# An opening gather of 128 slots instead of 256 in each expert layer, with the expert sort dealt out between its blocks

## The chip, the core and the metric

The program runs on one NeuronCore of a Trainium2 chip. The metric is the device time of one execution in microseconds (us), the median of several runs. Five engines work side by side: TensorE (PE, with its weight loads PEld), VectorE (DVE), ScalarE (ACT), GpSimd (POOL) and SyncE (SP), which issues nearly all DMA transfers.

## The reference, cut to what matters

The model has two transformer layers with attention and a mixture of experts, and then a third block of another kind. The change touches the two expert layers only. Layer 0 has 512 tokens, layer 1 has 256. Each token goes to 2 of 32 experts.

```python
grp   = argmax(g_logits)                         # one of 4 groups
top_p, top_i = top_k(softmax(e_logits[grp]), 2)  # two experts of that group
gate  = p_grp * top_p / sum(top_p)
...
xb = h_pad[slot_tok]                             # rows of tokens, expert by expert
yb = (silu(xb @ w1[e]) * (xb @ w3[e])) @ w2[e]   # D=1024, FF=512, float32
out[stok] += yb[dest] * sgate
```

The weights of an expert are 6 MB (w1, w3 and w2 of 2 MB each), and every expert is read once per layer: 192 MB a layer.

## The kernel before, in words

**Units.** `moe(l, Tn, ob)` handles one expert layer, with Tn = 4 or 2 tiles of 128 tokens. The 32 experts are packed into 14 units of 128 token slots: a unit of two experts has 64 slots for each, a unit of four has 32 for each. Units 0 and 1 hold the experts 0 to 3, which are fixed (`FIX = 4`). The experts of units 2 to 13 are placed by load: `sort_experts` ranks them by the number of their tokens, and the resulting ids (`eid`) are read by SP (`eid_at`, L862) to form the addresses of their weights. Unit 2 has four experts.

**Weights.** `Stream` lists 1 MB tiles in the order of use: w1 and w3 of unit 0 (8 tiles), w1 and w3 of unit 1 (8), w2 of unit 0 (4), w1 and w3 of unit 2 (16), w2 of unit 1 (4), and so on. They go through a ring of 12 tiles in layer 0 and 17 in layer 1. SP issues them in this order from L302; a tile can be issued when the tile that held its place has been multiplied. So the first tile whose address needs the sort is the 21st.

**Gather.** The rows of tokens are fetched by a product with a one-hot matrix: `onehot_tok(base)` writes `gr` (token x 256 slots, type fp32r), and `gather` multiplies it with the tokens `hs`, split into two fp32r parts `hi` and `lo`. The result is `xt`, 8 slices k of 128 features x 256 slots. For each k there are Tn x 2 matmuls with 128x128 weights (from `hs`) and 256 moving columns (from `gr`), accumulated in one PSUM bank for two slices, and ScalarE copies each bank to `xt` (L1100). One gather serves two units.

**The opening.** Before the first unit, `gather(gr0, blocks=(0, 1))` fills k = 0 to 3 for both units 0 and 1. `up` (L1216) multiplies `xt` with w1 of unit 0, slice by slice; in its middle, at k = 4, it calls the gather of k = 4 to 7 (pinned there by `late`). Then comes `overflow_slots`, a generator: its first part counts the tokens of each expert (L1157), runs `sort_experts` (L1136 to L1152) and stops at its `yield`; then `up` with w3 of unit 0; then its second part computes the final slots (L1165 to L1181). Units 1 to 13 follow, each with `up` for w1 and w3, and `down` (w2) and `combine` of the unit before it. Units 2, 4, 6, ... begin with a gather of 256 slots.

**Order.** The instructions of an engine run in program order. A planner makes that order from the order in which they are written and from its own estimate of when each is ready; `pin` fixes places by hand.

Of the kernel before, what the change touches and what calls it, by code (L numbers as in the profile page):

```python
# [163 lines left out]
def build(tc, A, out, stages=("A0", "M0", "A1", "M1", "F", "B"), dbg=None, inject=None):  # L164
# [22 lines left out]
    with es:  # L187
# [24 lines left out]
        def pin(i, on=True):  # L212
            return tc.keep_in_program_order(i) if on and i is not None else i
# [216 lines left out]
        def fill(n=1):  # L430
            for _ in range(n):
                if fills:
                    fills.pop(0)()
# [377 lines left out]
        def moe(l, Tn, ob):  # L811
# [78 lines left out]
            with sbuf(f"ringx{l}", nX, "right") as ringX, ExitStack() as mid, ExitStack() as early, ExitStack() as main:  # L890
# [13 lines left out]
                def sm(*shape, dt=F32, pool=M_):  # L904
                    cnt[0] += 1
                    return pool.tile([128] + list(shape), dt, name=f"s{cnt[0]}")
# [180 lines left out]
                        V.scalar_tensor_tensor(gr[:, t], C("iota"), sh[:, 1, t:t + 1], gr[:, t].bitcast(F32), op0=OP.is_equal, op1=OP.add)  # L1087
                    return gr

                def gather(gr, n=256, blocks=range(4), late=False):  # L1090
                    for b in blocks:
                        ps = PS()
                        for kk in range(2):
                            k = 2 * b + kk
                            o = ps[:, n * kk:n * kk + n]
                            for t in range(Tn):
                                h = hs[t // 2][:, t % 2, k]
                                pin(T.matmul(o, h.hi, gr[:, t, :n], start=(t == 0), stop=False), late and kk == t == 0)
                                T.matmul(o, h.lo, gr[:, t, :n], start=False, stop=(t == Tn - 1))
                        S.copy(xt[:, 2 * b:2 * b + 2, :n], ps[:, :2 * n].rearrange("p (k s) -> p k s", k=2))  # L1100

                gr0 = onehot_tok(0)
                gather(gr0, blocks=(0, 1))
                fill(100)
                W.pools, W.n = ringM, stream.done
                stream.upto(n2 + RN)

                gate, ex, den, ge, pg = sm(2, Tn), sm(Tn), sm(Tn), sm(Tn, 4), sm(Tn)
                pin(V.tensor_tensor(ge, g, gm[:, :, None].to_broadcast([128, Tn, 4]), op=OP.subtract))
                S.activation(ge, ge, AF.Exp)  # L1110
                V.tensor_reduce(pg, ge, axis=AX.X, op=OP.add)
                V.reciprocal(pg, pg)
                V.tensor_sub(m2, m2, m1)
                V.tensor_mul(m2, m2, gf)
                V.tensor_reduce(ex, m2, axis=AX.X, op=OP.add)
                S.activation(ex, ex, AF.Exp)
                V.tensor_scalar(den, ex, 1.0, None, op0=OP.add)
                V.reciprocal(den, den)
                V.tensor_mul(gate[:, 0], pg, den)
                V.tensor_mul(gate[:, 1], gate[:, 0], ex)  # L1120

                rowt = ob.tile([128, 2, 2, N], F32, name="rowt", tag="o")
                grow = sm(nC, D, pool=Z_)
                for c in range(nC):
                    modrow(grow[:, c], l, 5, c)

                cntc, ovc, cmp_, ovb = sm(1), sm(1), sm(nj), sm(3, 32)
                eid = lbx[:, 0:32].bitcast(I32)
# [4 lines left out]
                def sort_experts():  # L1133
                    T_ = C("tab")
                    ones, idn = C("ones"), ident[0:32, 0:32]
                    V.tensor_scalar(key[0:32], cntc[0:32], T_[0:32, 2:3], T_[0:32, 3:4], op0=OP.mult, op1=OP.add)  # L1136
                    pr = PS()
                    T.matmul(pr[0:32, 0:32], key[0:32].to_broadcast([32, 32]), idn, start=True, stop=True)
                    V.tensor_scalar(gt_[0:32], pr[0:32, 0:32], key[0:32], None, op0=OP.is_lt)
                    pr = PS()  # L1140
                    T.matmul(pr[0:32, 0:32], ones[0:32, 0:32], gt_[0:32], start=True, stop=True)
                    T.matmul(pr[0:32, 32:34], gt_[0:32], ones[0:32, 0:2], start=True, stop=True)
                    V.tensor_scalar(oh[0:32, 0], pr[0:32, 0:32], C("pcol")[0:32], None, op0=OP.is_equal)
                    V.tensor_scalar(oh[0:32, 1], C("iota32")[0:32], pr[0:32, 32:33], None, op0=OP.is_equal)
                    pr = PS()
                    T.matmul(pr[:, 0:32], C("pcol")[0:32].to_broadcast([32, 128]), oh[0:32, 1], start=True, stop=True)
                    for i in range(2):
                        T.matmul(pr[:, 32 + 32 * i:64 + 32 * i], T_[0:32, i:i + 1].to_broadcast([32, 128]), oh[0:32, 0], start=True, stop=True)
                    T.matmul(pr[0:32, 96:98], oh[0:32, 0], T_[0:32, 1:2].to_broadcast([32, 2]), start=True, stop=True)
                    V.tensor_copy(eid[0:1], pr[0:1, 0:32])  # L1150
                    V.tensor_copy(tabs, pr[:, 32:96].rearrange("p (a b) -> p a b", a=2))
                    V.tensor_copy(capc[0:32], pr[0:32, 96:97])  # L1152

                def overflow_slots():
                    pc = PS()
                    for t in range(Tn):
                        T.matmul(pc[0:32, 0:2], at_[:, t], C("ones")[:, 0:2], start=(t == 0), stop=(t == Tn - 1))  # L1157
                    V.tensor_copy(cntc[0:32], pc[0:32, 0:1])
                    sort_experts()
                    V.tensor_sub(cntc[0:32], cntc[0:32], capc[0:32])  # L1160
                    for j in range(nj):
                        V.tensor_scalar(cmp_[0:32, j:j + 1], cntc[0:32], float(128 * j), None, op0=OP.is_gt)
                    V.tensor_reduce(ovc[0:32], cmp_[0:32], axis=AX.X, op=OP.add)
                    yield
                    po = PS()  # L1165
                    for i, m in enumerate(("tri", "ident", "ones")):
                        T.matmul(po[:, 32 * i:32 * i + 32], ovc[0:32].to_broadcast([32, 128]), C(m)[0:32, 0:32], start=True, stop=True)
                    V.tensor_copy(ovb, po[:, 0:96].rearrange("p (a b) -> p a b", a=3))
                    V.tensor_sub(ovb[:, 0], ovb[:, 2], ovb[:, 0])
                    V.tensor_sub(ovb[:, 0], ovb[:, 0], ovb[:, 1])  # L1170
                    bx = gt_
                    V.tensor_scalar(bx, ovb[:, 0], 128.0, float(OVF), op0=OP.mult, op1=OP.add)
                    V.tensor_sub(bx, bx, tabs[:, 1])
                    pick(ek, tabs[:, 0, None, None, :].to_broadcast(wide))
                    pick(ovr, tabs[:, 1, None, None, :].to_broadcast(wide))
                    V.tensor_tensor(ovr, pk, ovr, op=OP.is_ge)
                    V.tensor_add(slot, ek, pk)
                    pick(bk, bx[:, None, None, :].to_broadcast(wide))
                    V.tensor_sub(bk, bk, ek)
                    V.tensor_mul(bk, bk, ovr)  # L1180
                    V.tensor_add(slot, slot, bk)  # L1181
                    debug(f"slot{l}", slot)

                def gate_rows():
                    for a, src in enumerate((slot, gate)):
# [20 lines left out]
                    V.scalar_tensor_tensor(sr, rowt[:, 0, 1], sid, s0, op0=OP.is_equal, op1=OP.add)  # L1206
                    return sr, gt[:, 2]

                def up(off, ws, mid=lambda: None):
                    ps = PS()  # L1210
                    m = 128 // len(ws)
                    for k in range(8):
                        if k == 4:
                            mid()
                        for q, w in enumerate(ws):
                            T.matmul(ps[m * q:m * q + m, :], xt[:, k, off + m * q:off + m * q + m], at(w, k)[k],  # L1216
                                     start=(k == 0), stop=(k == 7))
                    return ps
# [120 lines left out]
                for i in order + [None]:  # L1339
                    if i is not None:  # L1340
                        off = 128 * (i % 2)
                        if off == 0 and i != 0:
                            gather(onehot_tok(128 * i))
                        if i == 0:
                            p1 = up(off, ws[i][0], lambda: gather(gr0, blocks=(2, 3), late=True))
                            ov = overflow_slots()
                            next(ov)
                            p3 = up(off, ws[i][1])
                            next(ov, None)
                        if i > 1:  # L1350
                            sr, gt = scatter_mats(128 * i, i == last)
                        if i != 0:
                            p1 = up(off, ws[i][0])
                        if i == 1:
                            gate_rows()
                            pend[2:4] = scatter_mats(0)[::-1]
                            sr, gt = scatter_mats(128)
# [776 lines left out]
```

## Time and profile before

| | |
|---|---|
| median of 3 runs | 2079.9 us (2075.26 to 2083.57) |
| the profiled execution, its own time | 2082.3 us |
| its span, first to last instruction | 2080.6 us |
| mean granted TensorE clock | 0.975 |
| PE busy | 1944.3 us (93%) |
| DVE busy | 1076.9 us (52%) |
| ACT busy | 658.5 us (32%) |
| POOL busy | 475.8 us (23%) |
| moved by DMA | 585.44 MB |

The expert stage of layer 0 lies at about 318 to 780 us of the span, that of layer 1 at about 1051 to 1500. In a row of instructions the first number is the start in us, the second the duration, followed by engine, line, operation, result <- operands, shape and count; in brackets stands the idle time before it and what ended it. A float32 matmul appears as two records, an fp32r matmul as one. In a row of windows, each engine has its busy time and, in brackets, its instructions; then follow the granted clock (1.00 is 2.4 GHz, 0.50 is 1.2 GHz), the busy share of the 16 DMA engines, and GB/s.

### The profile page before, as it was taken

To read this page: it belongs to the slowest core of one execution; us is meant where nothing else is said; L and a number is where in the kernel's file an instruction comes from. 1 tells how busy PE (TensorE), PEld (TensorE's weight loads), DVE (VectorE), ACT (ScalarE), POOL (GpSimd) and SP (SyncE) were. 2 spreads that over 40 slices of the span, in tenths; PEclk is the share of its full clock that TensorE was granted. 3 is DMA by queue.
4 is the path that set the end of the run, shared out by engine and by line. 5 is a ranking of instruction groups with operands and counts; after the bars stand their busy time and mean duration, and the time that the engine had idled before them with its cause. 6 is when DMAs were issued, how large, how long until landed. Compare 5 with 4: busy or idle time off the path is not lost. (4 is left out here: it accounts for less than half of the span.)

```text
span 2080.6 us, 29614 instructions
## 1 busy us (share of the span) xinstructions
PE 1944.3 (93%) x11353; PEld 1229.8 (59%) x11353; DVE 1076.9 (52%) x1919; ACT 658.5 (32%) x1188; POOL 475.8 (23%) x365
## 2 busy tenths in 40 slices
PE   6999999999899998999899997999989999998997
PEld 3755574444344444677743332333379998988996
DVE  3476674454426566746643231233366775446553
ACT  3355531101001114446511010111164444455553
POOL 1234321121213123210111010011131440332331
PEclk7999999999999999999899999999999999999999
DMA  8573338999999996642389999999864453554552
GB/s 316 209 258 128 102 134 339 398 427 426 427 426 425 427 423 251 246 142 102 132 364 427 426 427 427 426 426 427 370 223 135 146 182 129 183 192 142 183 189 95
DMA packets 137794, 585.44 MB, mean 281 GB/s; under 512 B 17257, under 2 KB 21863, under 8 KB 88367
## 3 DMA queue, kind: packets, MB, share of 16 engines
q1 hardware_dynamic: 136798, 583.47, 71.8%
q8 instruction: 92, 1.51, 0.3%
q14 instruction: 56, 0.45, 0.1%
q10 hardware_dynamic: 848, 0.01, 0.0%
HBM read 582.33 MB, written 1.11 MB: 280 GB/s over the span
## 5 line engine op out<-in xcount | busy, mean ns | idle before, releaser
L1216 PE MATMUL ps<-w,xt 128*64 128x512 f32 (+1 forms) x2232 | 430.1, 612 | 23.7 <-DMA w<-expert_w 23.4
L269 DVE TENSOR_TENSOR spl<-w,sph 128x1024 fp32r<-128x1024 f32 (+1 forms) x153 | 203.8, 1335 | 193.8 <-ACT sph L266 192.7
L266 ACT CAST sph<-w 128x1024 fp32r<-128x1024 f32 (+1 forms) x204 | 213.0, 1045 | 282.0 <-PE pj L260 258.2
L1216 PEld LDWEIGHTS ps<-w,xt 128*64 128x64 f32 (+1 forms) x2232 | 125.6, 127 | 276.0 <-issue 225.1
L1271 DVE SCALAR_TENSOR_TENSOR t<-ps,gt,t 128x512 fp32r<-128x512 f32 x52 | 39.1, 751 | 474.7 <-ACT t L1270 473.0
L1255 PE MATMUL ps<-w,t 128*64 128x512 f32 (+1 forms) x1128 | 257.1, 604 | 16.3 <-DMA w<-expert_w 13.5
L1287 POOL TENSOR_TENSOR X<-X,tm 128x512 f32<-128x512 f32 x78 | 106.1, 1360 | 687.8 <-DVE tm L1286 686.5
L259 PE MATMUL pj<-hT2h,sph 128*128 128x256 f32 x864 | 241.0, 283 | 0.0
L260 PE MATMUL pj<-hT2l,sph 128*128 128x256 f32 x864 | 240.4, 280 | 0.0
L261 PE MATMUL pj<-hT2h,spl 128*128 128x256 f32 x864 | 239.2, 281 | 0.3 <-DVE spl L269 0.3
L269 POOL TENSOR_TENSOR spl<-w,sph 128x1024 fp32r<-128x1024 f32 (+1 forms) x51 | 126.5, 2481 | 340.1 <-ACT sph L266 339.7
L1270 ACT ACTIVATE t<-ps,gt 128x512 fp32r<-128x512 f32 x52 | 35.7, 687 | 515.6 <-PE ps L1255 513.0
L1255 PEld LDWEIGHTS ps<-w,t 128*64 128x64 f32 (+1 forms) x1128 | 82.2, 125 | 183.1 <-issue 131.9
L260 PEld LDWEIGHTS pj<-hT2l,sph 128*128 128x128 f32 x864 | 163.0, 189 | 0.8 <-issue 0.7
L259 PEld LDWEIGHTS pj<-hT2h,sph 128*128 128x128 f32 x864 | 162.3, 189 | 1.2 <-issue 0.7
L261 PEld LDWEIGHTS pj<-hT2h,spl 128*128 128x128 f32 x864 | 161.7, 188 | 0.6 <-DVE spl L269 0.5
L1280 PE MATMUL ps<-t,sr 128*128 128x512 f32 x336 | 96.0, 415 | 9.2 <-DVE t L1271 7.5
L1286 DVE TENSOR_TENSOR tm<-ps,s 128x512 f32<-128x512 f32 x156 | 101.9, 680 | 1.4 <-PE ps L1280 1.3
L1280 PEld LDWEIGHTS ps<-t,sr 128*128 128x128 f32 x336 | 60.1, 188 | 57.4 <-ACT t L1270 22.3
L445 PEld LDWEIGHTS ps<-c,t 128*128 128x128 f32 x496 | 56.1, 141 | 52.5 <-issue 20.0
L1287 DVE TENSOR_TENSOR X<-X,tm 128x512 f32<-128x512 f32 x78 | 85.6, 1097 | 1.9
L445 PE MATMUL ps<-c,t 128*128 128x128 f32 x496 | 76.2, 280 | 7.8 <-DVE t L1228 2.9
(509 smaller groups left out, 3394.1 us busy)
## 6 DMA issues: line engine op xcount, KB each, us to landing
w<-expert_w SPq DMA_DIRECT2D x372, 1024.0 KB
w<-ada_w SPq DMA_DIRECT2D x48, 1024.0 KB
w<-w_in SPq DMA_DIRECT2D x30, 1024.0 KB
w<-diff_w_in SPq DMA_DIRECT2D x12, 1024.0 KB
X<-expert_w SPq DMA_DIRECT2D x12, 1024.0 KB
w<-w_gate SPq DMA_DIRECT2D x12, 1024.0 KB
w<-w_ff_down SPq DMA_DIRECT2D x11, 1024.0 KB
w<-w_ff_gate SPq DMA_DIRECT2D x10, 1024.0 KB
```

Source lines behind the costliest of these rows:

```text
L259: T.matmul(o, l.hi, r.hi, start=start, stop=False, **kw)
L260: T.matmul(o, l.hi, r.lo, start=False, stop=False, **kw)
L261: T.matmul(o, l.lo, r.hi, start=False, stop=stop, **kw)
L266: pin(S.copy(d.hi, src), pinned)
L269: eng.tensor_tensor(d.lo, src, d.hi.bitcast(F32), op=OP.subtract)
L445: T.transpose(o, i, ident[:i.shape[0], :i.shape[0]])
L1216: T.matmul(ps[m * q:m * q + m, :], xt[:, k, off + m * q:off + m * q + m], at(w, k)[k], start=(k == 0), stop=(k == 7))
L1255: T.matmul(ps[m * q:m * q + m, :], hT_[:, k, m * q:m * q + m], at(w, k)[k, slice(512 * jo, 512 * jo + 512)], start=(k == 0), stop=(k == 3))
L1271: V.scalar_tensor_tensor(yl, ps, gt[:, 0:1], yh.bitcast(F32), op0=OP.mult, op1=OP.subtract)
L1280: T.matmul(ps, sr[:, 128 * t:128 * t + 128], ys[jo][q], start=(q == 0), stop=(q == 1))
L1286: V.tensor_mul(tmp, ps, grow[:, t // 2, cs])
L1287: (G if jo else V).tensor_add(X[:, t, cs], X[:, t, cs], tmp)
```

## The change

The opening gather is made in two parts of 128 slots. The first part, all eight slices k for the slots of unit 0, comes before the first `up`. The second part, all eight slices for the slots of unit 1, comes after `up` with w3 of unit 0. A bank now holds four slices of 128 slots, so a part has two blocks. The matmuls of both parts have 128 moving columns instead of 256. `up` loses its call in the middle.

`overflow_slots` starts before the gather. Its count and the first step of the sort come ahead of the first block; `sort_experts` now yields three times, and its second and third steps come after the first and the second block. The last step of the sort runs after `up` with w1, the final slots after `up` with w3, as before. The gate's computations keep their place behind the first gather. The later gathers, of 256 slots, are as they were.

```diff
-                def gather(gr, n=256, blocks=range(4), late=False):
-                    for b in blocks:
+                def gather(gr, n=256, lo=0, between=lambda: None):
+                    m = 512 // n
+                    for k0 in range(0, 8, m):
                         ps = PS()
-                        for kk in range(2):
-                            k = 2 * b + kk
+                        for kk in range(m):
                             o = ps[:, n * kk:n * kk + n]
                             for t in range(Tn):
-                                h = hs[t // 2][:, t % 2, k]
-                                pin(T.matmul(o, h.hi, gr[:, t, :n], start=(t == 0), stop=False), late and kk == t == 0)
-                                T.matmul(o, h.lo, gr[:, t, :n], start=False, stop=(t == Tn - 1))
-                        S.copy(xt[:, 2 * b:2 * b + 2, :n], ps[:, :2 * n].rearrange("p (k s) -> p k s", k=2))
-
-                gr0 = onehot_tok(0)
-                gather(gr0, blocks=(0, 1))
+                                h = hs[t // 2][:, t % 2, k0 + kk]
+                                T.matmul(o, h.hi, gr[:, t, lo:lo + n], start=(t == 0), stop=False)
+                                T.matmul(o, h.lo, gr[:, t, lo:lo + n], start=False, stop=(t == Tn - 1))
+                        S.copy(xt[:, k0:k0 + m, lo:lo + n], ps.rearrange("p (k s) -> p k s", k=m))
+                        between()
...
                     V.tensor_scalar(key[0:32], cntc[0:32], T_[0:32, 2:3], T_[0:32, 3:4], op0=OP.mult, op1=OP.add)
+                    yield
                     pr = PS()
                     T.matmul(pr[0:32, 0:32], key[0:32].to_broadcast([32, 32]), idn, start=True, stop=True)
                     V.tensor_scalar(gt_[0:32], pr[0:32, 0:32], key[0:32], None, op0=OP.is_lt)
+                    yield
                     pr = PS()
...
                     V.tensor_scalar(oh[0:32, 1], C("iota32")[0:32], pr[0:32, 32:33], None, op0=OP.is_equal)
+                    yield
                     pr = PS()
...
-                    sort_experts()
+                    yield from sort_experts()
...
+                gr0 = onehot_tok(0)
+                ov = overflow_slots()
+                next(ov)
+                gather(gr0, 128, 0, lambda: next(ov))
+                fill(100)
...
-                def up(off, ws, mid=lambda: None):
+                def up(off, ws):
                     ps = PS()
                     m = 128 // len(ws)
                     for k in range(8):
-                        if k == 4:
-                            mid()
...
                         if i == 0:
-                            p1 = up(off, ws[i][0], lambda: gather(gr0, blocks=(2, 3), late=True))
-                            ov = overflow_slots()
+                            p1 = up(off, ws[i][0])
                             next(ov)
                             p3 = up(off, ws[i][1])
                             next(ov, None)
+                            gather(gr0, 128, 128)
```

## Rows read from the trace of the kernel before

**Rows 1.** The page: DMA busy tenths in 40 slices of 52 us.
```profile
DMA  8573338999999996642389999999864453554552
```

**Rows 2.** Windows of layer 0's expert stage.
```profile
322.50:345.50 23.00, 22.09 (x137) 11.68 (x136) 3.31 (x20) 4.00 (x6) 0.00 (x0) 1.00 0.64 238
345.50:381.00 35.50, 35.21 (x198) 19.47 (x197) 24.79 (x53) 5.39 (x9) 7.78 (x8) 1.00 1.01 426
381.00:388.50 7.50, 7.50 (x69) 2.39 (x68) 6.15 (x13) 0.59 (x1) 6.12 (x5) 1.00 0.64 227
388.50:760.00 371.50, 353.38 (x1926) 155.49 (x1926) 172.62 (x257) 39.29 (x65) 74.51 (x58) 0.99 1.01 426
```

**Rows 3.** What SP waited for, 318 to 420 us: total, times, longest.
```profile
SPq L302 <- PE ps L1216: 40.0, 7, 18.5
SPq L862 <- DVE t L1152: 1.9, 1, 1.9
```

**Rows 4.** SP's issues of weight tiles in layer 0.
```profile
327.46 0.81 SPq L302 DMA_DIRECT2D w<-expert_w  x2
350.01 0.94 SPq L302 DMA_DIRECT2D w<-expert_w  x2
384.65 1.49 SPq L302 DMA_DIRECT2D w<-expert_w  x3
```

**Rows 5.** TensorE in order of time: layer 0's opening gather and first `up`.
```profile
318.27 0.39 PE L1098 MATMUL ps<-gr,hh0h 128*128 128x256 f32 x1 [1.98 <-DVE gr L1087]
323.79 3.65 PE L1216 MATMUL ps<-w,xt 128*64 128x512 f32 x16
327.37 0.39 PE L1098 MATMUL ps<-gr,hh0h 128*128 128x256 f32 x1
327.71 0.28 PE L1098 MATMUL ps<-gr,hh0h 128*128 128x256 f32 x1
331.19 0.28 PE L1099 MATMUL ps<-gr,hh1l 128*128 128x256 f32 x1
```

**Rows 6.** A window inside that gather's first part.
```profile
320.00:322.00 2.00, 2.00 (x11) 2.00 (x11) 0.00 (x0) 0.00 (x0) 0.00 (x0) 0.50 1.00 342
```

**Rows 7.** Weight loads and narrow float32 matmuls elsewhere, in order of time.
```profile
109.88 1.94 PEld L402 LDWEIGHTS ad<-c,R 128*128 128x128 f32 x16
...
113.59 0.64 PEld L405 LDWEIGHTS ad<-beta,rgw 128*36 128x36 f32 x16 [0.36 <-DVE rs L458]
...
961.37 1.06 PE L1492 MATMUL ps<-vd,t 128*128 128x128 f32 x8
```

**Rows 8.** TensorE during layer 0's sort.
```profile
335.33 0.24 PE L1138 MATMUL ps<-c,t 32*32 32x32 f32 x2
...
336.76 0.37 PE L1146 MATMUL ps<-t,c 32*128 32x32 f32 x2 [0.58 <-DVE t L1144]
...
337.66 7.09 PE L1216 MATMUL ps<-w,xt 128*64 128x512 f32 x32
```

**Rows 9.** POOL's one-hot for the second gather of layer 0.
```profile
349.48 3.62 POOL L1086 TENSOR_SCALAR gr<-c,sh 128x256 fp32r<-128x256 f32 x4 [31.23 <-DVE sh L1080]
```

**Rows 10.** Layer 1: windows.
```profile
1064.00:1072.00 8.00, 7.42 (x34) 2.98 (x35) 2.00 (x15) 0.01 (x1) 0.00 (x0) 0.79 0.31 98
...
1084.00:1480.00 396.00, 366.07 (x1877) 139.26 (x1874) 122.96 (x227) 45.25 (x75) 42.29 (x34) 0.99 1.01 426
```

**Rows 11.** Layer 1: TensorE and SP in order of time.
```profile
1051.70 0.39 PE L1098 MATMUL ps<-gr,hh0h 128*128 128x256 f32 x1 [1.00 <-DVE gr L1087]
...
1053.80 0.64 PE L1216 MATMUL ps<-X,xt 128*64 128x512 f32 x1
...
1065.63 8.78 PE L1216 MATMUL ps<-w,xt 128*64 128x512 f32 x32
...
1068.65 0.35 SPq L302 DMA_DIRECT2D w<-expert_w  x1
...
1075.12 7.09 PE L1216 MATMUL ps<-w,xt 128*64 128x512 f32 x32
```

More of the change, by code (lines that the diff above doesn't have):

```diff
@@ L1104, in moe @@
[L1104 to L1125, printed above, removed]
+                                h = hs[t // 2][:, t % 2, k0 + kk]
@@ L1182, in overflow_slots @@
                     debug(f"slot{l}", slot)
+                gr0 = onehot_tok(0)
[3 more added lines that the diff above has]
+                fill(100)
+                W.pools, W.n = ringM, stream.done
+                stream.upto(n2 + RN)
+                gate, ex, den, ge, pg = sm(2, Tn), sm(Tn), sm(Tn), sm(Tn, 4), sm(Tn)
+                pin(V.tensor_tensor(ge, g, gm[:, :, None].to_broadcast([128, Tn, 4]), op=OP.subtract))
+                S.activation(ge, ge, AF.Exp)
+                V.tensor_reduce(pg, ge, axis=AX.X, op=OP.add)
+                V.reciprocal(pg, pg)
+                V.tensor_sub(m2, m2, m1)
+                V.tensor_mul(m2, m2, gf)
+                V.tensor_reduce(ex, m2, axis=AX.X, op=OP.add)
+                S.activation(ex, ex, AF.Exp)
+                V.tensor_scalar(den, ex, 1.0, None, op0=OP.add)
+                V.reciprocal(den, den)
+                V.tensor_mul(gate[:, 0], pg, den)
+                V.tensor_mul(gate[:, 1], gate[:, 0], ex)
+                rowt = ob.tile([128, 2, 2, N], F32, name="rowt", tag="o")
+                grow = sm(nC, D, pool=Z_)
+                for c in range(nC):
+                    modrow(grow[:, c], l, 5, c)
                 def gate_rows():
```

## The prediction

> **What bounds the kernel now.** I read the page's slices first. DMA is at nine tenths or more through both expert stages (slices 7 to 15 and 21 to 28), except where a stage opens [rows 1]. The windows show the same finely. In layer 0 the DMA engines are busy 0.64 of the stretch from 322.5 to 345.5, then fully to 381, 0.64 again to 388.5, and from there 1.01 at 426 GB/s to 760 [rows 2]. So they stand still 23 x 0.36 = 8.3 us and 7.5 x 0.36 = 2.7 us, and after that the stage runs at the speed of the weights. Layer 1 stands 8 x 0.69 = 5.5 us at its opening and is then full to 1480 [rows 10]. Any us by which the last of these standstills ends later moves the whole rest of the kernel, as nothing behind it can catch up.
>
> Next I asked what ends the standstills: the waits of SP. In layer 0 it waited 40.0 us for w1/w3 matmuls (L1216) and only 1.9 us for the sorted ids (L862) [rows 3]. The ring of 12 tiles is full when the stage opens, so a tile is issued when `up` has used one: two at 327.46, just as the first half of `up` ends, and three at 384.65, in unit 2's w1 [rows 4, 5]. Between 345.5 and 381 TensorE is busy 35.21 of 35.50 us [rows 2]. The chain that sets layer 0's end is therefore TensorE's own work from 318.27 to about 384.5, and from there DMA. The sort is not on it as a result, only as time that TensorE spends.
>
> In layer 1 the ring of 17 tiles reaches further. SP issued at 1068.65, shortly after the sort ended and w3 began at 1065.63 [rows 11]; there the ids do play a part, next to the ring.
>
> **The gather, the large term.** Before, layer 0's opening has 8 slices x 4 token tiles x 2 parts = 64 matmuls of 256 columns: 32 from 318.27 to 323.79, 5.52 us, and 32 from 327.37 to about 331.4, 4.0 us [rows 5]. In the second set the 3rd starts at 327.71 and the 32nd at 331.19, so 3.48 / 29 = 0.120 us apart. The first set is 1.7 us longer than 32 x 0.120, as it ran partly at a granted clock of 0.50, which is 1.2 GHz, after TensorE had waited for `gr` [rows 5, 6]; I leave that loss in.
>
> After, it has 128 matmuls of 128 columns: each half needs its own pass over all the weights of `hs`. Layer 1 has half of everything, 64 for 32.
>
> What does a 128-column fp32r matmul cost? No row shows one: the trace's fp32r matmuls move 256 columns or more. So, bounds.
> - Below: loading 128x128 four-byte weights for only 2 columns takes 1.94 / 16 = 0.12 us, and with 36 columns of weights 0.64 / 16 = 0.04 [rows 7]. The load is paid by weight columns, and `hs` still has 128. So I see no reason for less than 0.12, the price of the 256-column matmul now. If this load were hidden after all, half of 0.120 is the floor: 0.06.
> - Above: the products of 128x128 weights with 128 columns that the trace does have are plain float32, two records each. Eight records took 1.06 us; with 0.28 for the last one's own length as in [rows 5], starts are 0.111 apart, and a product costs 0.22. With no overlap at all it is 1.06 / 4 = 0.265.
>
> The first bound has the right type and the wrong width, the second the right width and the wrong type. I take 0.22: it is the only price that the trace shows for this shape, and nothing in it shows that the single-pass rate of fp32r is kept below 256 columns. It is my least certain choice, so the other end gets a large chance below.
>
> The Trainium skill has a rule that speaks against the change at either price: the page "TensorE: Matmul & The Clock Gate", section "LDWEIGHTS (loading the stationary operand)", prices a weight load by its columns, about columns / 1.2 ns, whatever follows. That would be 107 ns here; the rows say 120, so they agree. By its figure the 64 added loads of layer 0 would take 6.8 us, by the row 7.7.
>
> Layer 0: added 128 x 0.223 = 28.5, plus the half-clock loss of 1.7, less 5.5 + 4.0: **+20.7 us** on TensorE's chain. The place of the second part doesn't matter for the sum, as both lie before 384.65. The four copies by ScalarE stay four of the same size, and `up` can start on the first block while the second is copied.
>
> **The sort.** Before, TensorE spends 335.33 to 337.66 = 2.33 us on it, mostly waiting for VectorE's small steps [rows 8]. After, the first two steps lie between gather blocks of 32 matmuls, which cover VectorE's part; their matmuls remain, some 0.5 us. The last step still stands behind `up` with w1: 336.76 to 337.66, 0.9 us [rows 8]. Saved: about **0.9 us** per layer. The count moves into TensorE's idle 1.98 us ahead of the gather [rows 5]. If VectorE's one-hot work delays these steps, the cover is lost and the 0.9 with it. The ids are ready no earlier in layer 0, since the longer gather comes first; the first tile to need them is the 21st, issued at 350.01, long after them [rows 4], so SP's queue waits for nothing new.
>
> `gr` has one buffer and is now held until the second part is done. Behind it waits POOL's one-hot for unit 2, 3.62 us from 349.48 [rows 9], with VectorE's additions. It would start near 364 and is needed near 392: hidden, with over 20 us to spare.
>
> Layer 0 in sum: 20.7 - 0.9 = **+19.8 us**.
>
> **Layer 1.** Removed: 16 matmuls from 1051.70 to 1053.80 [rows 11], 2.1 us, and as many again inside `up`: 4.2. Added: 64 x 0.223 = 14.3. Sort: -0.9. Further, `up` with w3 took 8.78 us where layer 0's took 7.09 [rows 8, 11], with a granted clock of 0.79 in that stretch [rows 10], after TensorE had waited in the sort; with shorter waits I give back 1.7. So unit 1's w1 starts 14.3 - 4.2 - 0.9 - 1.7 = 7.5 us later. DMA sees less of it. From 1068.65 five tiles followed, up to about 1081 (2.46 us each at 426 GB/s), while the sixth needs the first half of unit 1's w1: 1075.12 + 3.55 = 1078.7 before, in time; 1086.2 after. It restarts some **5.3 us** later than 1081 and is full from there.
>
> **Sum.** 19.8 + 5.3 = 25.1 us on the profiled execution's own 2082.3: 2107.4. That execution lies 2.4 above the median of the runs, so on the median's scale 2105, +1.2%. A change under 0.5% (10.4 us) can't be told from none here.
>
> **Rivals.**
> 1. *The narrow matmul costs what the wide one does, 0.12, being bound by its weight load.* For it: the loads [rows 7], and the same type. Layer 0: 128 x 0.120 = 15.4, + 1.7 - 9.5 - 0.9 = +6.7. Layer 1: TensorE 7.7 - 4.2 - 0.9 - 1.7 = +0.9, while `up` with w1 runs undivided, so w3's first tiles come free about 1.5 us earlier and DMA restarts earlier by that. Together +5: 2085, no measurable change. It decides below a price of 0.15.
> 2. *Narrow is really cheaper.* At 0.06, layer 0 gives 7.7 + 1.7 - 9.5 - 0.9 = -1.0 and layer 1 3.8 - 4.2 - 2.6 = -3.0: 2076. Against it: the loads [rows 7]. The skill's same page, section "Back-to-back issue gap", gives 81 ns per matmul in a stream of weight loads and 128-column matmuls; by that estimate layer 0 is +1.7 and layer 1 -1.6, about 2080. No row here shows it.
> 3. *The sort does bind, and earlier ids start the loads: faster.* The place is SP, L862. If the ids were what ends the standstills, up to 8.3 + 2.7 + 5.5 = 16.5 us could go: 2063. It needs more than 10.4 of them. Against it: 40.0 us of waits for L1216 to 1.9 for the ids [rows 3], and the longer first gather. For it: only layer 1's first tile at 1068.65 [rows 11].
>
> **Chances.** Forecast 0.62; rival 1 0.24; rival 2 0.08; rival 3 0.04; 0.02 for something slower still. Below, the range takes in rival 1 with the 5 us by which single runs lie under the median, 2080; above, it takes a product of 0.265 (128 x 0.04 and its share in layer 1, some 7 us): 2112. The forecast's own range is 2099 to 2112. Slower by over 0.5%: the forecast and the rest, with a little of rival 1, 0.65. Within 0.5%: 0.31. Faster: 0.04.
>
> **What the profile after would show.** The starts of the gather's 128-column matmuls 0.22 apart, or 0.12; that one figure decides. Layer 0's unit 2 starting near 401 instead of 381, and the three tiles of 384.65 issued some 20 us later; a second DMA standstill before unit 1's w1 in both layers; full DMA after that; PE waits in the sort gone but for its last step. Wrong would make it: the planner moving the second part away, a low clock through the whole first part, or slack behind 388 that I don't see.

## The result and the profile after

The changed kernel takes 2098.95 us (median of 8 runs, 2088.51 to 2105.39), the kernel before 2080.65 us (8 runs, 2075.26 to 2083.57): a ratio of 1.0088, 95% interval 1.0071 to 1.0106. It is slower by 18.3 us. The forecast was 2105, range 2080 to 2112. The direction and the range hold (2098.95 is just under the forecast's own range of 2099 to 2112), but the profile shows that the price on which the sum was built is not what happened.

The profiled execution of after took 2093.48 us, span 2091.8 us. First the page: the granted clock and DMA in 40 slices of 52 us. DMA answers to [rows 1].

```profile
PEclk9999998999999998999889999999989999999999
DMA  8673336999999996733289999999964453554652
```

The seventh slice, 314 to 366 us, is where layer 0's expert stage opens: DMA is at 6 there, where it was at 8, and the clock at 8. The clock has eights again where layer 1 opens, in the 20th and 21st slice. How much is lost and to what has to be read instruction by instruction. This is TensorE's timeline of after at layer 0's opening and at the second part, the answer to [rows 5]:

```profile
317.77 0.33 PE L1098 MATMUL ps<-gr,hh0h 128*128 128x128 f32 x1 [1.61 <-DVE gr L1087]
...
319.37 0.27 PE L1099 MATMUL ps<-gr,hh1l 128*128 128x128 f32 x1
319.48 0.28 PE L1098 MATMUL ps<-gr,hh0h 128*128 128x128 f32 x1
...
324.01 0.41 PE L1099 MATMUL ps<-gr,hh1l 128*128 128x128 f32 x1
324.22 0.41 PE L1098 MATMUL ps<-gr,hh0h 128*128 128x128 f32 x1
...
329.77 5.97 PE L1220 MATMUL ps<-w,xt 128*64 128x512 f32 x16
...
336.23 3.65 PE L1220 MATMUL ps<-w,xt 128*64 128x512 f32 x16
...
348.09 0.33 PE L1098 MATMUL ps<-gr,hh0h 128*128 128x128 f32 x1
...
355.39 1.08 PE L1220 MATMUL ps<-w,xt 128*64 128x512 f32 x4
...
391.23 1.06 PE L1220 MATMUL ps<-w,xt 128*32 128x512 f32 x8
```

Read the starts, not the durations, which overlap. At 319.4 two narrow matmuls start 0.11 us apart, at 324 they start 0.21 us apart: the same instruction at two prices. The second part, 348.09 to 355.39, takes 7.3 us; the first, with as many matmuls and a few small ones of the sort, 11.4 us from 317.77 to its last start at 329.13. Sixteen records, that is eight float32 matmuls, of `up` took 5.97 us from 329.77 and 3.65 us from 336.23. The windows of after say why. They stand in the form of [rows 2]; the first group has four of 4 us, the second the standstills of DMA.

```profile
320.00:324.00 4.00, 4.00 (x24) 4.00 (x24) 0.00 (x0) 0.39 (x1) 0.00 (x0) 0.60 0.72 264
324.00:328.00 4.00, 4.00 (x20) 4.00 (x21) 0.00 (x0) 0.19 (x1) 0.00 (x0) 0.50 0.01 3
328.00:332.00 4.00, 4.00 (x18) 2.41 (x19) 1.14 (x7) 0.80 (x2) 0.00 (x0) 0.50 0.02 4
332.00:336.00 4.00, 4.00 (x15) 1.18 (x11) 0.00 (x0) 0.00 (x0) 0.00 (x0) 0.69 0.00 0
...
322.00:336.00 14.00, 14.00 (x59) 9.59 (x58) 1.14 (x7) 1.39 (x3) 0.00 (x0) 0.55 0.07 27
336.00:358.00 22.00, 22.00 (x137) 12.76 (x138) 7.08 (x31) 3.05 (x4) 2.45 (x3) 1.00 0.96 381
358.00:360.00 2.00, 2.00 (x16) 1.00 (x12) 1.44 (x4) 0.34 (x1) 1.17 (x2) 1.00 0.07 21
390.00:394.00 4.00, 4.00 (x39) 2.03 (x42) 3.90 (x8) 0.65 (x2) 3.04 (x2) 1.00 0.39 166
394.00:398.00 4.00, 4.00 (x41) 1.04 (x32) 3.41 (x7) 0.00 (x0) 3.34 (x4) 1.00 0.54 154
398.00:760.00 362.00, 342.82 (x1884) 150.43 (x1882) 165.57 (x248) 36.80 (x61) 73.92 (x56) 0.99 1.01 426
```

TensorE is busy without a gap from 320 to 336 and runs at a granted clock of 0.50, that is 1.2 GHz, for most of it. The clock was at 1.00 up to 320; TensorE had waited 1.61 us for `gr` just before the gather. The clock came back to 1.00 in the middle of the first `up`. Unit 2's w1 starts at 391.23. DMA stands still for 14 x 0.93 = 13.0 us there, 1.9 at 358 and 4.0 x 0.61 + 4.0 x 0.46 = 4.3 in unit 2, against 8.3 and 2.7 before, and is full from 398, where before it was full from 388.5. What ends the standstills is as before: SP's waits from 318 to 420, the same stretch as in [rows 3], and its first issues of weight tiles behind the first, the second and the third standstill.

```profile
SPq L302 <- PE ps L1220: 58.1, 9, 27.3
...
SPq L862 <- DVE s L1139: 0.5, 1, 0.5
```

```profile
335.77 0.81 SPq L302 DMA_DIRECT2D w<-expert_w  x2
...
359.36 0.94 SPq L302 DMA_DIRECT2D w<-expert_w  x2
...
394.88 5.24 SPq L302 DMA_DIRECT2D w<-expert_w  x8
```

The first issue moves from 327.46 to 335.77, the last from 384.65 to 394.88 [rows 4]: 10.2 us. Layer 1 opens with the same picture, shorter. Windows of 4 us of after, two from its gather's start at 1065.97 and then four for DMA:

```profile
1065.97:1069.97 4.00, 3.98 (x28) 3.87 (x28) 0.37 (x2) 0.59 (x1) 0.00 (x0) 0.80 1.01 426
1069.97:1073.97 4.00, 4.00 (x18) 2.46 (x19) 1.11 (x7) 2.08 (x3) 0.00 (x0) 0.50 1.00 424
...
1072.00:1076.00 4.00, 4.00 (x12) 1.08 (x12) 1.02 (x7) 1.68 (x3) 0.00 (x0) 0.60 0.79 331
1076.00:1080.00 4.00, 4.00 (x22) 1.57 (x20) 0.00 (x0) 0.00 (x0) 0.00 (x0) 1.00 0.49 138
1080.00:1084.00 4.00, 4.00 (x22) 1.48 (x20) 1.61 (x13) 0.60 (x1) 0.00 (x0) 1.00 0.32 133
1084.00:1088.00 4.00, 4.00 (x22) 1.29 (x19) 0.00 (x0) 0.00 (x0) 0.00 (x0) 1.00 0.60 180
```

From 1072 to 1088 DMA stands for 4 x (0.21 + 0.51 + 0.68 + 0.40) = 7.2 us, against 5.5 before [rows 10]. In TensorE's timeline the gather starts behind a wait of 0.79 us, and `up` with w3 takes 7.09 us where it took 8.78 [rows 11]:

```profile
1065.99 0.33 PE L1098 MATMUL ps<-gr,hh0h 128*128 128x128 f32 x1 [0.79 <-DVE gr L1087]
...
1081.66 7.09 PE L1220 MATMUL ps<-w,xt 128*64 128x512 f32 x32
```

### The profile page after: what moved, and what is told of

It reads as the page before. It is cut to its first block, busy times and chain, and to the rows that moved or that the text cites. A ratio compares the mean times of both kernels' runs of the same rounds, so it can differ in the third digit from the quotient of the medians.

```text
span 2091.8 us, 29805 instructions
## 1 busy us (share of the span) xinstructions
PE 1959.9 (94%) x11449; PEld 1241.7 (59%) x11449; DVE 1076.5 (51%) x1919; ACT 658.5 (31%) x1188; POOL 475.7 (23%) x365
## 5 line engine op out<-in xcount | busy, mean ns | idle before, releaser
L445 PEld LDWEIGHTS ps<-c,t 128*128 128x128 f32 x496 | 55.8, 141 | 53.3 <-issue 20.6
```

What stands on the lines that cost most here:

```text
L445: T.transpose(o, i, ident[:i.shape[0], :i.shape[0]])
```

## The experiments

Theory after this reading: a narrow matmul costs its weight load, 0.11 us at 2.4 GHz, so the split alone adds some 6 us in layer 0; the rest of the 18 us is TensorE at 1.2 GHz in the openings, because the clock falls around the wait for `gr` and the narrow gather does not get it back. Rivals: the narrow stream is slow in itself, wherever it stands; the dealt sort costs, by holding up the gather; it is the split's order (two parts, two standstills) and not the width.

All kernels keep the whole computation; where work is added, it is said. The table gives for each its median, the ratio to the kernel before, measured beside it, with its 95% interval, and three readings of its profiled execution: the time from the first gather matmul of layer 0 to the first w1 matmul of unit 2, and the time at 1.2 GHz within 20 us of the gather's start in layers 0 and 1. For these I took ten windows of 2 us and summed 4 us x (1 - granted clock). (The 3.4 us of before in layer 1 lie behind the sort, in `up` with w3, and not in the gather.)

| kernel | median us | ratio | gather to unit 2, us | 1.2 GHz, layer 0 | layer 1 |
|---|---|---|---|---|---|
| before | 2080.65 | | 62.7 | 3.4 | 3.4 |
| after | 2098.95 | 1.0088 [1.0071, 1.0106] | 73.5 | 13.7 | 6.8 |
| after_again | 2098.92 | 1.0086 [1.0062, 1.0109] | 75.0 | 17.1 | 6.8 |
| sort_only | 2075.68 | 0.9977 [0.9966, 0.9987] | 61.4 | 3.4 | 0 |
| split_only | 2093.62 | 1.0058 [1.0040, 1.0076] | 74.5 | 13.6 | 6.8 |
| wide_twice | 2084.13 | 1.0011 [0.9999, 1.0022] | 69.3 | 3.4 | 0 |
| first_wide | 2085.05 | 1.0028 [1.0012, 1.0043] | 68.8 | 3.4 | 0 |
| whole_first | 2075.14 | 0.9975 [0.9965, 0.9986] | 61.6 | 3.4 | 0 |
| after_fill | 2081.59 | 1.0009 [0.9996, 1.0023] | 66.9 | 0 | 0 |
| narrow_fill | 2078.99 | 0.9989 [0.9974, 1.0004] | 66.7 | 0 | 0 |
| whole_fill | 2075.65 | 0.9973 [0.9963, 0.9984] | 60.4 | 0 | 0 |
| split0_only | 2092.82 | 1.0051 [1.0039, 1.0063] | 74.9 | 17.1 | 0 |
| split1_only | 2078.06 | 0.9983 [0.9970, 0.9995] | 61.6 | 3.4 | 6.8 |
| whole_fill0 | 2074.15 | 0.9956 [0.9942, 0.9970] | 60.4 | 0 | 0 |

The 62.7 us of before run from 318.27 [rows 5] to this row:

```profile
381.00 7.07 PE L1216 MATMUL ps<-w,xt 128*32 128x512 f32 x64
```

**The two halves of the change.** sort_only deals the sort out between the gather's blocks and leaves the gather as it was, with 256 columns and its second half inside `up`:

```diff
-                gather(gr0, 128, 0, lambda: next(ov))
+                gather(gr0, blocks=(0, 1), between=lambda: next(ov))
...
-                            p1 = up(off, ws[i][0])
+                            p1 = up(off, ws[i][0], lambda: gather(gr0, blocks=(2, 3), late=True))
...
-                            gather(gr0, 128, 128)
```

> The sort dealt out between the gather's blocks as in the changed kernel, the gather itself as before (256 columns, second half inside the first up). Theory (narrow matmuls pay a full weight load and leave TensorE at 1.2 GHz for long): the split gather is the whole cost, so this is level with before or 1 to 3 us faster, 2078 to 2081. Rival (the sort's new place costs, because VectorE's steps now stand between gather blocks and the ids come late): 5 us or more slower, 2086 or above.

split_only has the gather in two narrow parts and the whole sort behind `up` with w1, as before:

```diff
-                ov = overflow_slots()
-                next(ov)
-                gather(gr0, 128, 0, lambda: next(ov))
+                gather(gr0, 128, 0)
...
                             p1 = up(off, ws[i][0])
-                            next(ov)
+                            ov = overflow_slots()
+                            for _ in range(4):
+                                next(ov)
```

> The gather in two parts of 128 slots, the sort in its old place behind the first up. Theory: the cost of the changed kernel is here, plus the 1 us per layer that the dealt sort saves: 2098 to 2103. Rival (the sort's place costs): about 2085 or less.

With the gather as it was, dealing the sort out gives 5 us: the rival that the sort holds up the gather falls there. The split alone loses 13, so most of the loss is the split's. Both results lie on the fast side of the theory's ranges, by 2 and by 4 us, and the two don't add up: 13 - 5 would be 8, and after loses 18. I had put split_only above after, and it is 5.3 us below.

The clock goes with this difference. Every execution has its mean granted clock on record: 0.973 on the average over the 6 of split_only, 0.970 over the 14 of after and after_again. As time at 1.2 GHz (twice the span, times 1 - clock) that is 113 and 125 us, and half of the difference is 6 us. But the single executions overlap (0.969 to 0.978, and 0.966 to 0.977). That the dealt sort lowers the clock of the narrow gather is therefore not shown, and neither is how it would.

**Width or order.** wide_twice keeps the two parts and their places, but both multiply all 256 columns and copy only the half that is wanted, so twice the columns for the same result:

```diff
+                def gather_wide(gr, half, between=lambda: None):
...
+                                T.matmul(o, h.hi, gr[:, t], start=(t == 0), stop=False)
+                                T.matmul(o, h.lo, gr[:, t], start=False, stop=(t == Tn - 1))
+                        lo = 128 * half
+                        S.copy(xt[:, 2 * b:2 * b + 2, lo:lo + 128], ps.rearrange("p (k s) -> p k s", k=2)[:, :, lo:lo + 128])
```

> As the changed kernel, but each matmul of both parts has 256 columns (twice the columns, the same number of weight loads; only the wanted half is copied, in eight copies instead of four). Theory (width sets how long the clock stays at 1.2 GHz): faster than the changed kernel although it computes more, about 2092 to 2095, with the low clock over in layer 0 before the first up. Rival (only the added weight loads cost, the clock is an accident): 0.120 for 0.112 us in 192 matmuls, 1.5 us slower than the changed kernel, 2100 or above.

whole_first has one gather of 256 slots ahead of the first `up`, with the sort's steps behind the first two of its four blocks:

```diff
-                gather(gr0, 128, 0, lambda: next(ov))
+                nx = [0, 0, 1, 1]
+                gather(gr0, between=lambda: next(ov, None) if nx.pop() else None)
...
-                            gather(gr0, 128, 128)
```

> One gather of 256 slots, all of it ahead of the first up, the sort dealt between its blocks: no added weight load, but the first up starts as late as with the split. Theory (added loads and clock are the cost): level with before, 2077 to 2082. Rival (the first tiles of the ring come free later and the longer standstill of DMA at the opening is the cost): 4 us or more slower, 2085 or above.

Twice the columns, in the same order, are 15 us faster than after, where my theory had 4 to 7. The order is not it, and at a full clock the width has hardly a price: less half of its 3.4 us at 1.2 GHz, wide_twice's way to unit 2 is 67.6 us, and that of after_fill below, at a full clock with 128 columns, 66.9. At 1.2 GHz it has none: two starts of wide_twice's gather there are 0.21 us apart, as in after. Windows of wide_twice over the same stretch follow.

```profile
320.04 0.42 PE L1111 MATMUL ps<-gr,hh0h 128*128 128x256 f32 x1
320.25 0.42 PE L1112 MATMUL ps<-gr,hh0l 128*128 128x256 f32 x1
```

```profile
316.00:320.00 4.00, 2.39 (x17) 2.02 (x15) 2.49 (x8) 0.00 (x0) 1.46 (x2) 0.80 1.00 421
320.00:324.00 4.00, 4.00 (x29) 4.00 (x28) 0.00 (x0) 0.37 (x1) 0.00 (x0) 0.77 0.73 262
324.00:328.00 4.00, 4.00 (x35) 3.65 (x36) 0.29 (x2) 1.12 (x3) 0.00 (x0) 1.00 0.01 3
328.00:332.00 4.00, 4.00 (x22) 1.35 (x20) 0.85 (x6) 0.21 (x1) 0.00 (x0) 1.00 0.02 4
```

The clock falls here as well, ahead of 320, but it is back before 324. whole_first does without the second pass over the weights and is another 9 us faster, 2 us below its range.

first_wide uses `gather_wide` for the first part and keeps the second narrow:

```diff
-                gather(gr0, 128, 0, lambda: next(ov))
+                gather_wide(gr0, 0, lambda: next(ov))
```

> The first part with 256 columns (half of them thrown away), the second part narrow. Theory (only the first part's narrow matmuls hold the clock down; behind a warm start narrow ones cost their weight load, 0.112 us): about the time of the version with both parts wide, 2081 to 2086. Rival (each narrow part costs its share whatever the clock): half of the loss stays, 2089 to 2093.

It is like wide_twice (2085.05 and 2084.13; 68.8 and 69.3 us to unit 2). In the medians a narrow second part costs nothing against a wide one: it comes behind `up`, the clock is high, and it stays high through it, as in after from 348 to 355. So it is the narrow gather that comes behind a wait which loses, and the rival of a stream that is slow in itself falls. (Three of first_wide's 12 executions took 2092 to 2095 us at mean clocks of 0.970 to 0.973, below the 0.975 of all twelve; none of wide_twice's took over 2088.2. The profile isn't one of the three, so where they lost their clock is open.)

**The wait ahead of the gather.** after_fill is after with three more dummy matmuls in layer 0 and one in layer 1, in TensorE's idle time before the gather. They are the kernel's own float32 dummies of 256 columns, of which four stood there already:

```diff
-                busy(4, at_.rearrange("p t e -> p (t e)"))
+                busy(7 - 2 * l, at_.rearrange("p t e -> p (t e)"))
```

> The changed kernel with three more (layer 1: one more) of the dummy matmuls that stand ahead of the gather, so that TensorE's wait for the one-hot is filled. Theory A (the idle time lets the clock fall, the narrow matmuls only fail to raise it): the low stretch is gone and about 6 us in layer 0 and up to 3 in layer 1 with it, 2088 to 2092. Theory B (the narrow stream lets it fall by itself): no gain, 2097 to 2101.

after_again is after itself, measured beside after_fill.

> The changed kernel itself once more, for a second profile beside the next three. Theory (narrow matmuls don't lift the clock): again 10 us or more at 1.2 GHz after the start of layer 0's gather, and 2095 to 2102. Rival (the low clock of the first profile was an accident of that execution): a stretch of 3 to 4 us as in the kernel before, and a time that differs with it.

The same code with a few dummies is 17.3 us faster, as fast as before; theory A had the direction, with half the size. after_again came as expected. This is TensorE's timeline of after_fill at the gather's start, and two windows:

```profile
314.22 3.27 PE L426 MATMUL ad<-c,s 128*128 128x256 f32 x14
317.42 0.41 PE L1136 MATMUL ps<-c,s 128*32 128x2 f32 x8
318.03 0.33 PE L1098 MATMUL ps<-gr,hh0h 128*128 128x128 f32 x1 [0.20 <-DVE s L1137]
```

```profile
320.00:324.00 4.00, 4.00 (x37) 3.89 (x37) 0.24 (x1) 0.59 (x1) 0.00 (x0) 1.00 0.82 287
324.00:328.00 4.00, 4.00 (x32) 2.77 (x33) 1.14 (x7) 0.80 (x2) 0.00 (x0) 1.00 0.02 8
```

The wait is 0.20 us instead of 1.61, and the clock stays at 1.00: 37 and 32 matmuls in four us where after had 24 and 20. Is it the gap, or must the filling be of wide float32 work? narrow_fill fills it with the gather's own kind, 14 matmuls of 128 fp32r columns in layer 0 and 8 in layer 1:

```diff
+                psn = PS("ad")
+                for _ in range(14 if l == 0 else 8):
+                    pin(T.matmul(psn[:, 0:128], hs[0].hi[:, 0, 0], hs[0].hi[:, 0, 1], start=True, stop=True))
```

> The changed kernel, with TensorE's wait ahead of the gather filled by narrow matmuls of 128 columns (14 in layer 0, 8 in layer 1) in place of the wide f32 dummies. If it is the idle gap that drops the clock, any work cures it: full clock in both openings, 2081 to 2085 us. If only wide work holds the clock up ahead of the narrow gather: half clock through the first part, 2092 us or more.

```profile
314.54 1.78 PE L1067 MATMUL ad<-hh0h 128*128 128x128 f32 x14
316.22 0.33 PE L1101 MATMUL ps<-gr,hh0h 128*128 128x128 f32 x1
```

```profile
316.00:320.00 4.00, 4.00 (x36) 3.85 (x36) 0.98 (x4) 0.00 (x0) 0.00 (x0) 1.00 1.01 384
320.00:324.00 4.00, 4.00 (x39) 3.93 (x38) 0.00 (x0) 0.65 (x2) 0.00 (x0) 1.00 0.36 144
```

These are TensorE's timeline and two windows of narrow_fill. 1.78 us of narrow work hold the clock as well as the wide dummies do. In layer 0 it is the gap that matters, not the kind of work that fills it. The median, 2078.99, is 2 us below the range. (The gather of this execution starts at 316.22 rather than near 318, but the work ahead of it ran 1.6 us earlier already, so that is no gain of the filling. One of its 12 executions took 2092.91 us, at the lowest clock of the twelve, 0.974.)

In layer 1 the gap alone is not enough. whole_fill0 below opens it with a wide gather behind the same wait of 0.79 us, unfilled, and with the same 6.8 us at 1.2 GHz a little earlier. Its clock stays at 1.00 through the gather, where after's fell to 0.50 some 2 us into it:

```profile
1047.65 0.39 PE L1098 MATMUL ps<-gr,hh0h 128*128 128x256 f32 x1 [0.79 <-DVE gr L1087]
```

```profile
1040.00:1044.00 4.00, 4.00 (x12) 1.66 (x10) 3.87 (x23) 0.48 (x2) 0.68 (x1) 0.60 1.01 424
1044.00:1048.00 4.00, 3.21 (x20) 2.09 (x20) 3.04 (x13) 0.00 (x0) 0.99 (x1) 1.00 1.01 422
1048.00:1052.00 4.00, 4.00 (x36) 3.68 (x35) 1.35 (x8) 1.80 (x4) 0.00 (x0) 1.00 1.01 428
```

So in layer 1 the wait and the narrow gather act together. after_fill shortened that wait only from 0.79 to 0.63 us and its clock stayed at 1.00, but it had no low stretch ahead of the gather either; how much of the cure there is the filling's is not shown.

**What a full clock is worth to the wide gather.** whole_fill is whole_first with the filling of after_fill; whole_fill0 has it in layer 0 alone (`busy(4 if l else 7, ...)`).

> One gather of 256 slots ahead of the first up with the sort dealt between its blocks, and TensorE's wait for the one-hot filled with dummy matmuls. Theory (the low clock at the opening costs 1.7 us in layer 0 even with wide matmuls): 1 to 3 us faster than the same without the filling, 2072 to 2074. Rival (the dummies delay the gather or the clock falls all the same): 2075 to 2078.

> The whole gather ahead of the first up, the sort dealt out, and the three more dummy matmuls in layer 0 alone. If a full clock in layer 0's opening is worth anything where the gather is wide: 2072 to 2075 us. If the wide gather lifts the clock soon enough by itself: 2075 to 2076, as without the dummies.

The 3.4 us at 1.2 GHz go in layer 0, and the way to unit 2 falls from 61.6 to 60.4 us, but the medians hardly differ: 2075.14, 2075.65 and 2074.15. whole_fill misses its theory's range and lies in the rival's, though not for the rival's reason, as the clock did not fall. A wide gather gets its clock back by itself. whole_fill0 is the fastest of the study, 0.44% below before by its ratio; whether the filling has a share in that can't be told from whole_first.

**Which layer.** split0_only has the narrow parts in layer 0 and whole_first's gather in layer 1, split1_only the reverse:

```diff
-                gather(gr0, 128, 0, lambda: next(ov))
+                nx = [0, 0, 1, 1]
+                if l == 0:
+                    gather(gr0, 128, 0, lambda: next(ov))
+                else:
+                    gather(gr0, between=lambda: next(ov) if nx.pop() else None)
```

> The gather in two narrow parts in layer 0 alone; layer 1 opens with its whole gather. Theory (the loss is weight loads, which only layer 0 pays in full, plus TensorE's low clock in the opening, of which layer 0 has the longer stretch): 6.5 us of weight loads and about 9 us of clock on 2075, 2088 to 2092 us. Rival (both layers lose alike): 2087 or less, with the layer-1 run of the same call as high.

> The gather in two narrow parts in layer 1 alone; layer 0 opens with its whole gather. Theory: few more weight loads there and a half clock that costs about 5 us, 2079 to 2084 us. Rival (both layers lose alike): 2087. If layer 1 lost only because layer 0 had run late: 2075 to 2077.

Against whole_first's 2075.14, layer 0 loses 17.7 us and layer 1 2.9 (by the ratios, which allow for the kernel before being 1 us slower beside these two, 16 and 2). Both lie 1 us outside their ranges. Layer 1's clock was low for 6.8 us in split1_only though layer 0 had run at its best, so its loss is its own; in the medians it is smaller than the 5 us that the theory gave it, while in the profiles layer 1 is 5.0 us longer than whole_first's (457.5 against 452.5, from its gather to its last `down`). Layer 0's loss is larger than what I gave it, in an execution that was at 1.2 GHz for 17.1 us rather than 13.7. The two add up to 20.6, to 2095.7; after is 3.2 above, which these runs don't place.

## Why the prediction was right, and where its working was not

**What binds: right.** The standstills at the opening end when `up` frees the ring, and everything behind moves with them. SP waits longer for w1/w3 matmuls (58.1 us against 40.0) and less for the ids (0.5 against 1.9). One wait of before is missing from [rows 3]: 7.2 us of L302 that ended with L1138, the sort's first matmul, which stands right behind `up`. It is no wait for the ids, which come of L1152; in sort_only it is gone, SP waits 4.5 us for the ids there, and the kernel is faster. In the first 84 us from the gather's start the four windows from 0, 4, 28 and 60 us hold 29.8 MB before and 25.3 MB after; the 4.5 MB missing are 10.7 us at 426 GB/s. The second standstill ahead of unit 1's w1 is there.

**The price of a narrow matmul: wrong.** This is the step that failed: "I take 0.22". At 2.4 GHz the starts are 0.111 us apart, which is rival 1's bound, the weight load. The measured price is below its decision point of 0.15, and its forecast, 2085 and no measurable change, is near what after_fill shows at a full clock: 2081.59. (60.4 us to 66.9 from whole_fill to after_fill is +6.5; 128 x 0.1115 - 64 x 0.120 = 6.6.) Unit 2 started at 391.23, not near 401. I had taken the price of the float32 row, in which a matmul is two records, for the price of its width. The trace's own row of 128x128 loads for two columns, 0.12 us [rows 7], was the right one: the load, not the columns, sets the pace. In after_fill's window from 320 to 324 the loads (PEld) fill 3.89 of the 4.00 us. The Trainium skill, page "TensorE: Matmul & The Clock Gate", section "LDWEIGHTS (loading the stationary operand)", gives 107 ns for 128 columns, and the measured 0.111 at 2.4 GHz agrees within 4%; at 1.2 GHz the measured 0.213 is twice that. The 81 ns that I had cited from its section "Back-to-back issue gap" appear in no run here.

**What filled the place of the price: the clock.** I named "a low clock through the whole first part" among what would make the forecast wrong, and carried the 1.7 us lost to it before [rows 5, 6] as a constant. That loss came of 3.4 us at 1.2 GHz; they grew to 13.7 and 17.1 us in the two profiled executions of after. By the table, half of 13.7 is 6.9 us of TensorE's time, and after's way to unit 2 is 73.5 - 66.9 = 6.6 longer than after_fill's; for after_again, half of 17.1 is 8.6 and the way is 8.1 longer. At 1.2 GHz the starts are 0.213 apart, by chance nearly my 0.22, and only in part of the gather. That the range holds is luck in this: a wrong price stood in for a loss that I had called a sign of being wrong. The whole account in medians: before 2080.65; the sort dealt out -5 (sort_only, whole_first); the split at a full clock +6 (whole_fill to after_fill); the low clock +17.3 (after_fill to after_again). The openings do not hold all of the last term. The mean clocks of all executions do: 0.9785 over the 12 of after_fill and 0.9698 over the 6 of after_again are 89 and 126 us at 1.2 GHz, and half of the 37 between them is 18.5. The profiles of after_again place 17.1 + 6.8 of them behind the two gathers and 6.8 ahead of layer 1's.

**Layer 0 and layer 1.** Forecast +19.8 and +5.3. From the gather's start to the last matmul of the last `down` layer 0 grew by 12.2 us in the profiled execution (476.6 to 488.8) and by 13.6 in after_again; the time on to layer 1's gather, for which the forecast has no term, grew by 2.6 and 2.2, and layer 1 by the same measure by 1.4 (455.8 to 457.2) and 1.3. The last block, which the change doesn't touch, then took 4.5 us less in the profiled after and 0.5 less in after_again, so the first profile shows the loss too small. I had layer 1's 1.7 us of half clock given back, and `up` with w3 did so; but 6.8 us at 1.2 GHz came ahead of it. DMA's standstill there grew by 1.7 us, not 5.3 (by its own figures, 1086.2 - 1081, 5.2). In sum 16 and 17 us of the 18.3 are seen in the expert layers and between them.

**The sort.** Forecast -0.9 us a layer; measured -5 in all. The way to unit 2 shortens by 1.3 us (62.7 to 61.4), near the 0.9. From the gather to the last `down` sort_only's layers are 3.0 and 2.0 us shorter than before's (473.6 and 453.8). In layer 0 the rest is the clock again, at the far end: the 32 records of the last `down` take 7.14 us in sort_only and 8.83 in before, which is 1.7 us. In layer 1 both take 8.83; what gains the 2.0 there I did not follow to its cause.

**The one-hot for unit 2: right.** It started at 355.55 on POOL (364 forecast), well ahead of unit 2's gather, and no wait for it appears:

```profile
355.55 3.61 POOL L1086 TENSOR_SCALAR gr<-c,sh 128x256 fp32r<-128x256 f32 x4 [38.06 <-PE ps L1099]
```

**What stays open.** In layer 1 seven of the fourteen profiled executions are at 1.2 GHz for 6.8 us in the 12 us ahead of the gather, all four with unfilled narrow parts there among them, but three with wide ones too; I have no account of that. Why the narrow gather keeps the low clock that it meets is not shown. split_only's median is 5.3 us below after's though it lacks the dealt sort, which gains 5 with a wide gather; the mean clocks go with that and do not explain it. The executions of after spread over 17 us, and their mean clocks, from 0.966 to 0.977, follow their times: together with after_again's, the two slowest have 0.966 and 0.967 and the two fastest 0.977.

## What to carry to other kernels

Halving the columns of these matmuls from 256 to 128, with a stationary tile that stays 128 wide, halved nothing (0.120 to 0.111 us): the load sets the pace, and a split in two pays it twice. Price a shape that the trace doesn't show by the row that shares its bound, not by the one that shares its outline. And read the granted clock around each wait of TensorE before moving work there: waits of 1.6 and 0.8 us ahead of two narrow gathers were worth 17 us of 2099, and under two us of useless matmuls in each took that away.

## What the runs showed of the hardware

- A matmul of 128 fp32r columns with a 128x128 weight load starts every 0.111 us at 2.4 GHz and every 0.213 us at 1.2 GHz; with 256 columns it is 0.12 at 2.4 GHz and 0.21 at 1.2 GHz (wide_twice, 320.04 to 321.54).
- In after TensorE was busy 4.00 of 4.00 us in the windows from 320 to 336 and stayed at 1.2 GHz to about 334, some 9 us of narrow gather and 5 us of float32 `up`. The same narrow stream from 348 to 355, entered at 2.4 GHz, stayed there. The six unfilled wide gathers of layer 0 came back to 2.4 GHz after 3.4 us. The Trainium skill, page "TensorE: Matmul & The Clock Gate", section "What's actually happening", has the clock fall when TensorE has been idle and rise when it has been busy. The four kernels whose wait is filled in layer 0 bear out the first half, as their clock did not fall; the second does not hold for the narrow stream in after, which these windows call busy throughout.
